# Expert weights in 2 KB packets, experts of the groups in turn, two scatters in flight

## The chip, the cores and the metric

The kernel runs on one core of one Trainium2 chip. The metric is the time of one execution on the device in microseconds (us). The profile is of one execution, taken by the hardware profiler; its times are microseconds from the span's start. PE is TensorE's matrix multiply, PEld its weight load, DVE is VectorE, ACT is ScalarE, POOL is GpSimd, SP is SyncE, which issues the ordinary DMAs; SPq and POOLq are sequencers. The core has 16 DMA engines, on which the DMAs of every issuing engine run: queue q1 holds what SP issues (plain loads and stores), q0 what GpSimd issues (indirect gathers and scatters).

## The reference

A decoder block on 1024 tokens of width 1024: a norm, a projection, stick-breaking attention beside a gated short convolution, merged and projected back, and then a mixture of experts. Only the last part is touched:

```python
def hierarchical_moe(h, w_rg, b_rg, w_re, b_re, w_gate, w_up, w_down):
    g_logits = hf @ w_rg + b_rg
    g_prob = jax.nn.softmax(g_logits, axis=-1)
    _, g_idx = lax.top_k(g_logits, 1)
    ...
    e_in_group = jnp.take_along_axis(e_logits, g_idx[:, :, None], axis=1)[:, 0]
    top_v, top_i = lax.top_k(e_in_group, TOP_K_IN_GROUP)
    ...
    for g in range(N_GROUPS):
        sl = slice(g * EXPERTS_PER_GROUP, (g + 1) * EXPERTS_PER_GROUP)
        act = silu(einsum('nd,edf->nef', h, w_gate[sl])) * einsum('nd,edf->nef', h, w_up[sl])
        act = act * combine[:, g, :, None]
        y = y + jnp.einsum('nef,efd->nd', act, w_down[sl])
```

There are 4 groups of 8 experts. A token takes one group and two experts in it, so that experts of different groups never share a token, while two of one group may. Gate and up are [1024, 256] each for an expert, down is [256, 1024], all float32: 3 MB an expert, 100 MB in all.

## The kernel before

Everything up to the merge is left as it is. The stages that matter begin at about 690 us.

**Output projection, second norm, routing** (from line 769). Eight tiles of 128 tokens. Tiles 0 to 5 run whole and end with `finish(t)` (L995): `add_x` adds the product to the residual rows XR[t % 3] on VectorE, `norm2` works out the norm's factor in small steps on GpSimd (L190 to L197), and `put_x(t, half)` (L866) multiplies one half of the row with the norm's gain into the buffer HX on GpSimd (L868) and issues two stores on SP: HX into the table h2d in DRAM (L869), XR into the output (L870). Tiles 6 and 7 run by column halves (L1020): `add_x` and `put_x` come after each half, and `norm2(6, G)` stands on GpSimd behind `put_x(6, 1)`. `tr_x`, `route`, `rank` and `table` (L880 to L956), spread over the products of later tiles, transpose the rows, choose group and experts, and build the slot tables: for each expert up to SLOTS = 88 rows with their token numbers. L1063 and L1064 turn them into `idx`; a slot without a token points to one of 128 rows past the output's end (`dumpc`, L780).

**Weight loads.** An expert has six chunks of 512 KB: four with 256 rows of gate and of up (two loads of 256 KB, L803), two with 128 rows of down (one load of 512 KB, L805). `chunks` (L790) fixes their order. `load_upto` (L807) issues loads on SP into a ring of some 39 buffers, CH, which come free one after the other as earlier stages end; in the expert loop a chunk is loaded again into a buffer once it has been split (L1112). A gate or up load takes rows i * 256 to i * 256 + 255: one contiguous run of 256 KB, which goes to the partitions in pieces of one row, 1 KB. A piece of down is 4 KB. A piece is a packet in the profile.

**Experts** (L1084 to L1198). Experts run in the order of their number. `gather(e)` fetches the expert's rows from h2d by `idx` (GpSimd, L1093). `xT` transposes them (PE L1134) and splits them in a high and a low part. `split_chunk` (L1100) splits each chunk alike: ScalarE copies the high part (L1103), VectorE subtracts (L1104). `expert_mm` does three products of 512 columns for each pair of parts (through `mm`, L124). `gateup(e)` runs four chunks, calls `aT(e - 1)`, `xT(e + 1)` and `gather(e + 3)` between them and ends with the activation; `down(e - 1)` follows, copies its result into one of two buffers YE (L1174) and issues the scatter that adds its rows to the output in DRAM (GpSimd, L1178). All scatters write the same tensor, so each waits on GpSimd until the one before has landed.

A loop for tokens past an expert's first 88 slots ends the kernel (L1212). With these inputs it runs no pass.

Of the kernel before, what the change touches and what calls it, by code (L numbers as in the profile page):

```python
# [40 lines left out]
class Order:  # L41
    """Puts steps given in a plain sequential order into the order in which to issue them: a step
    comes once what it reads is there and what it overwrites is read, the longest chain first."""
# [55 lines left out]
def tile_hybrid_block(  # L99
# [34 lines left out]
    def warm(n):  # L134
        """Products that nothing reads, to keep the array's clock up where it would idle."""
        for _ in range(n):
            mm(PS[:, 1, :], onesB, onesB[:, None, :].to_broadcast([128, 4, 128]), True, True)

    # ------------------------------------------------------------------ constants
# [62 lines left out]
    # ------------------------------------------------------------------ weights of three column blocks  # L202
# [35 lines left out]
    # ------------------------------------------------------------------ first norm, transposed  # L238
# [148 lines left out]
    def unit(n, u):  # L387
# [26 lines left out]
        def scan():  # L414
            P = PT[nP]
            # a first row block's last 128 keys of a diagonal unit are all masked
# [17 lines left out]
        for sp in range(w // 256):  # L434
            tr, x = 4 + state["sp"] % 2, state["sp"] % 3
            state["sp"] += 1
            # quarters (key block, row block); the masked one of a diagonal unit is zero
# [143 lines left out]
    # ------------------------------------------------------------------ transposed blocks of the other projections  # L581
# [186 lines left out]
    # ------------------------------------------------------------------ output projection, second norm, routing  # L768
# [11 lines left out]
    dumpc = rc.tile([128, 1], F32, name="dumpc")  # L780
    G.iota(dumpc, pattern=[[0, 1]], base=N + 1, channel_multiplier=1, allow_small_or_imprecise_dtypes=True)
# [7 lines left out]

    chunks = []  # L790
# [8 lines left out]
    def load_chunk(r, i, wg, wu, wd, Y=Y):  # L799
        if i < 4:  # L800
            v = r.rearrange("p (k j c) -> p k j c", k=2, j=2)
            for j, w in enumerate((wg, wu)):
                Y.dma_start(v[:, :, j], w[i * 256:(i + 1) * 256].rearrange("(k p) c -> p k c", p=128))  # L803
        else:
            Y.dma_start(r, wd[(i - 4) * 128:(i - 3) * 128])  # L805

    def load_upto(n, ring=0, Y=Y):  # L807
        while lst["n"] < min(n, len(chunks)):
            e, i = chunks[lst["n"]]
            load_chunk(CH[lst["n"] % (ring or len(chunks))], i, w_gate_e[0, e], w_up_e[0, e], w_down_e[0, e], Y)  # L810
# [55 lines left out]
    def put_x(t, half):  # L866
        tsl, hs = slice(t * 128, (t + 1) * 128), slice(half * 512, (half + 1) * 512)
        G.tensor_mul(HX[:, hs], XR[t % 3][:, hs], g2[:, hs])  # L868
        Y.dma_start(h2d[tsl, hs], HX[:, hs])  # L869
# [17 lines left out]
    def route(t):  # L887
# [27 lines left out]
        # combine weights times the norm's factor  # L915
# [103 lines left out]
    # the last two tiles by column halves  # L1019
# [41 lines left out]
    # slot tables  # L1061
    t2 = sm.tile([128, NE], F32, name="t2")
    V.tensor_scalar(t2[0:SLOTS], TAB[:, 0:NE], 0.0, dumpc[0:SLOTS], op0=OP.is_equal, op1=OP.mult)  # L1063
# [3 lines left out]
    # tiles past the first of each expert, as a running count  # L1067
# [15 lines left out]
    # ------------------------------------------------------------------ experts  # L1083
# [8 lines left out]
    def gather(e):  # L1092
        G.indirect_dma_start(out=XE[e % 2][:, :], out_offset=None, in_=h2d[:, :],  # L1093
                             in_offset=bass.IndirectOffsetOnAxis(ap=idx[0:SLOTS, e:e + 1], axis=0),
# [19 lines left out]
    def expert_mm(e, i, xt, at, o):  # L1114
        wh, wl = split.pop((e, i))
        if i < 4:
            for kk in range(2):
                k = 2 * i + kk
                cs = slice(kk * 512, (kk + 1) * 512)
                mm3(o, xt[0][:, k], xt[1][:, k], wh[:, cs], wl[:, cs], k == 0, k == 7)  # L1120
# [17 lines left out]
    pos = {"n": 0}  # L1138

    def gateup(e):  # L1140
# [14 lines left out]
        S.activation(sg, o[:, 0:DE], AF.Silu, scale=rsl[0:SLOTS, e:e + 1])  # L1155
        V.scalar_tensor_tensor(ac, o[:, DE:2 * DE], wsl[0:SLOTS, e:e + 1], sg, op0=OP.mult, op1=OP.mult)
# [10 lines left out]
    def down(e):  # L1167
# [10 lines left out]
        G.indirect_dma_start(out=out[:, :], out_offset=bass.IndirectOffsetOnAxis(ap=idx[0:SLOTS, e:e + 1], axis=0),  # L1178
# [101 lines left out]
```

## Time and profile before

| | us |
|---|---|
| runs | 1200.8, 1202.41, 1202.41 |
| median | 1202.41 |
| the profiled execution's span | 1199.3 |

| engine | busy us of the span | share |
|---|---|---|
| PE (products) | 1114.5 | 93% |
| PEld (weight loads) | 893.6 | 75% |
| DVE | 757.6 | 63% |
| ACT | 644.9 | 54% |
| POOL | 363.0 | 30% |

The profile has 149666 DMA packets with 169.18 MB, of which 129097 packets are under 2 KB. The span is the time from the first to the last event of the profiled execution; the runs are timed on their own. Busy shares are means over stages with different limits; what binds one stage is read in that stage. The DMA share is the time of all packets over the time of 16 engines, so that packets that overlap on an engine can bring it above 1.

### The profile page before, as it was taken

To read this page: it belongs to the slowest core of one execution; us is meant where nothing else is said; L and a number is where in the kernel's file an instruction comes from. 1 tells how busy PE (TensorE), PEld (TensorE's weight loads), DVE (VectorE), ACT (ScalarE), POOL (GpSimd) and SP (SyncE) were. 2 spreads that over 40 slices of the span, in tenths; PEclk is the share of its full clock that TensorE was granted. 3 is DMA by queue.
4 is the path that set the end of the run, shared out by engine and by line. 5 is a ranking of instruction groups with operands and counts; after the bars stand their busy time and mean duration, and the time that the engine had idled before them with its cause. 6 is when DMAs were issued, how large, how long until landed. Compare 5 with 4: busy or idle time off the path is not lost.

```text
span 1199.3 us, 16771 instructions
## 1 busy us (share of the span) xinstructions
PE 1114.5 (93%) x5761; PEld 893.6 (75%) x5761; DVE 757.6 (63%) x1317; ACT 644.9 (54%) x1204; POOL 363.0 (30%) x658
## 2 busy tenths in 40 slices
PE   6999898999999999999999999998899999899883
PEld 5988897987888888888888887786566656566552
DVE  5579989989885332333324073445598889688772
ACT  6586767777653213222223142223588878687672
POOL 4636466463000000000000004555363334333211
PEclk9999999998999999999999999999899999899897
DMA  6000101011011111111121168928899999999993
GB/s 222 27 27 14 40 2 40 15 29 34 1 36 54 53 36 45 53 53 52 37 62 45 36 189 290 322 73 276 241 316 312 323 323 292 310 314 317 328 322 82
DMA packets 149666, 169.18 MB, mean 141 GB/s; under 512 B 14381, under 2 KB 129097, under 8 KB 149577
## 3 DMA queue, kind: packets, MB, share of 16 engines
q1 hardware_dynamic: 140360, 148.12, 38.2%
q0 software_dynamic: 9216, 19.95, 7.7%
q8 instruction: 46, 0.75, 0.2%
q14 instruction: 44, 0.35, 0.1%
HBM read 150.72 MB, written 20.45 MB: 143 GB/s over the span
## 4 chain that ended last, share of the span: by engine, by line
PE 52%; DMA 27%; DVE 8%; issue 5%; POOL 4%; ACT 2%; SPq 1%; POOLq 0%; DVEq 0%; ACTq 0%
PE PS L124 49%; DMA out_dram<-xr,idx 10%; DMA out_dram<-ye,idx 8%; DVE pt L421 3%; PE PS L446 2%; DMA cha<-in_w_down_e_dram 2%; DMA xr<-h2d,idx 1%; DMA chr<-in_w_up_e_dram 1%; DVE WL L231 1%; DVE ahl L466 1%; POOL hx L868 1%; PE PS L338 1%; DMA chr<-in_w_down_e_dram 1%; DMA mg<-in_w_down_e_dram 1%; DMA h2d<-hx 1%
## 5 line engine op out<-in xcount | busy, mean ns | idle before, releaser
L124 PE MATMUL PS<-hH,WH 128*128 128x512 f32 x448 | 143.9, 394 | 1.1 <-DVE attF L478 1.1
L124 PE MATMUL PS<-hH,WL 128*128 128x512 f32 x448 | 142.0, 390 | 0.0
L124 PE MATMUL PS<-hL,WH 128*128 128x512 f32 x448 | 141.9, 389 | 0.0
L124 PE MATMUL PS<-WH,xet 128*88 128x512 f32 x384 | 137.9, 410 | 3.5 <-ACT WH L1103 3.5
L421 DVE TENSOR_TENSOR_SCAN pt<-pt 128x128 f32<-128x128 f32 (+2 forms) x96 | 92.8, 1008 | 18.5 <-issue 13.4
L674 POOL TENSOR_TENSOR mg<-mg,sga 128x1024 f32<-128x1024 f32 x6 | 14.7, 2456 | 293.0 <-DVE sga L672 293.0
L124 PEld LDWEIGHTS PS<-hH,WL 128*128 128x128 f32 x448 | 84.1, 188 | 17.7
L124 PEld LDWEIGHTS PS<-hH,WH 128*128 128x128 f32 x448 | 84.1, 188 | 17.4 <-ACT WH L610 1.2
L124 PEld LDWEIGHTS PS<-hL,WH 128*128 128x128 f32 x448 | 84.2, 188 | 16.4
L124 PE MATMUL PS<-WH,hH 128*128 128x384 f32 x256 | 91.9, 359 | 4.4 <-ACT hH L268 2.3
L611 DVE SCALAR_TENSOR_TENSOR WL<-br,cols,WH 128x128 fp32r<-128x128 f32 x200 | 68.9, 411 | 29.3 <-ACT WH L610 29.3
L124 PE MATMUL PS<-WH,hL 128*128 128x384 f32 x256 | 87.2, 341 | 0.0
L124 PE MATMUL PS<-WL,hH 128*128 128x384 f32 x256 | 86.8, 339 | 0.0
L615 DVE TENSOR_TENSOR WL<-br,WH 128x512 fp32r<-128x512 f32 x16 | 11.1, 691 | 116.5 <-ACT WH L614 116.5
L610 ACT ACTIVATE WH<-br,cols 128x128 fp32r<-128x128 f32 x200 | 65.4, 392 | 35.6 <-PE PS L124 34.4
L124 PE MATMUL PS<-WL,xet 128*88 128x512 f32 x192 | 79.2, 413 | 4.9 <-DVE WL L1104 4.4
L124 PEld LDWEIGHTS PS<-WH,xet 128*88 128x88 f32 x384 | 61.3, 160 | 29.5 <-ACT WH L1103 4.1
L124 PE MATMUL PS<-WH,act 128*88 128x512 f32 x192 | 65.5, 395 | 1.2 <-ACT act L1164 1.2
L1178 POOL DMA_INDIRECT out_dram<-xr,idx x16 | 35.2, 2200 | 100.7 <-DMA out_dram<-ye,idx 56.0
L460 POOL CAST ahl<-zeros 128x256 fp32r<-128x256 f32 x32 | 30.4, 958 | 115.5 <-PE PS L124 107.0
L124 PE MATMUL PS<-ahl,vt 128*128 128x256 f32 x320 | 53.7, 298 | 11.4 <-DVE attF L478 10.7
L1178 POOL DMA_INDIRECT out_dram<-ye,idx x16 | 31.5, 1970 | 99.6 <-DMA out_dram<-xr,idx 75.7
(278 smaller groups left out, 2726.2 us busy)
## 6 DMA issues: line engine op xcount, KB each, us to landing
br<-in_w_in_dram SPq DMA_DIRECT2D x25, 512.0 KB
cha<-in_w_gate_e_dram SPq DMA_DIRECT2D x42, 256.0 KB
cha<-in_w_up_e_dram SPq DMA_DIRECT2D x42, 256.0 KB
cha<-in_w_down_e_dram SPq DMA_DIRECT2D x18, 512.0 KB
mg<-in_w_down_e_dram SPq DMA_DIRECT2D x17, 512.0 KB
mg<-in_w_gate_e_dram SPq DMA_DIRECT2D x29, 256.0 KB
mg<-in_w_up_e_dram SPq DMA_DIRECT2D x29, 256.0 KB
br<-in_w_in_dram SPq DMA_DIRECT2D x36, 192.0 KB
```

The source lines that it names most:

```text
L124: T.matmul(o, a, b, start=start, stop=stop)
L231: V.scalar_tensor_tensor(WL3[:, k], WR[idx, k // 2][:, k % 2], g1[:, k:k + 1], WH3[:, k], op0=OP.mult, op1=OP.subtract)
L338: T.transpose(pb[:, j].bitcast(F32R), st[:, a, j * 128:(j + 1) * 128], identR)
L421: V.tensor_tensor_scan(pr, pr, pr, 1.0 if diag else P[:, j, w:w + 1], op0=OP.mult, op1=OP.bypass)
L446: T.transpose(PS[:, tr, q * 128:(q + 1) * 128], BT[n % 3][:, j, (sp * 2 + sj) * 128:(sp * 2 + sj + 1) * 128], identF)
L460: G.tensor_copy(AHL[x][:, :, 0:128], zeros[:, None, :].to_broadcast([128, 2, 128]))
L466: V.tensor_sub(AHL[x][:, 1, lo:512], PS[:, tr, lo:512], AHL[x][:, 0, lo:512])
L610: S.activation(j.wH[:, k], r[:, k], AF.Copy, scale=g1[:, k:k + 1])
L611: V.scalar_tensor_tensor(j.wL[:, k], r[:, k], g1[:, k:k + 1], j.wH[:, k], op0=OP.mult, op1=OP.subtract)
L674: (G if b < 6 else V).tensor_add(mg, mg, mst[b].rearrange("p (t c) -> p t c", c=128))
L868: G.tensor_mul(HX[:, hs], XR[t % 3][:, hs], g2[:, hs])
L1178: G.indirect_dma_start(out=out[:, :], out_offset=bass.IndirectOffsetOnAxis(ap=idx[0:SLOTS, e:e + 1], axis=0), in_=ye[:, :], in_offset=None ...
```

## The change

1. A gate or up load now takes two neighbouring rows for each partition: partition p holds rows 8p to 8p + 7, chunk i rows 8p + 2i and 8p + 2i + 1. A piece is 2 KB, and the pieces of a load lie 8 KB apart in DRAM. The columns of h2d are stored in the matching order (k, p) in place of (p, k), so that `xT` still takes 128 neighbouring columns. In `put_x` both products on GpSimd come with the second half, read in steps of 8 elements, and one store writes the whole row. In the chunk gate and up lie as (j k c), and a product reads gate and up of one k as two runs of 256 columns.
2. Experts run in the order EX: one of group 0, one of group 1, 2, 3, then the second of each group, and so on. Slots without a token point into one half or the other of the spare rows, by the parity of the group, so that neighbouring scatters share no row.
3. The dependency of a scatter on the one just before is taken away, and one on the scatter two before is set. Ahead of the last four a memset of one element stands on GpSimd.

The rest of the diff takes comments out and follows the new names.

```diff
-    dumpc = rc.tile([128, 1], F32, name="dumpc")
-    G.iota(dumpc, pattern=[[0, 1]], base=N + 1, channel_multiplier=1, allow_small_or_imprecise_dtypes=True)
+    dumpc = rc.tile([128, 2], F32, name="dumpc")
+    G.iota(dumpc[:, 0:1], pattern=[[0, 1]], base=N + 1, channel_multiplier=1, allow_small_or_imprecise_dtypes=True)
+    G.iota(dumpc[0:64, 1:2], pattern=[[0, 1]], base=N + 65, channel_multiplier=1, allow_small_or_imprecise_dtypes=True)
+    G.iota(dumpc[64:128, 1:2], pattern=[[0, 1]], base=N + 1, channel_multiplier=1, allow_small_or_imprecise_dtypes=True)
...
+    EX = [(n % 4) * 8 + n // 4 for n in range(NE)]
...
         if i < 4:
-            v = r.rearrange("p (k j c) -> p k j c", k=2, j=2)
+            v = r.rearrange("p (j k c) -> p j k c", k=2, j=2)
             for j, w in enumerate((wg, wu)):
-                Y.dma_start(v[:, :, j], w[i * 256:(i + 1) * 256].rearrange("(k p) c -> p k c", p=128))
+                Y.dma_start(v[:, j], w.rearrange("(p k) c -> p k c", k=8)[:, 2 * i:2 * i + 2])
...
-        G.tensor_mul(HX[:, hs], XR[t % 3][:, hs], g2[:, hs])
-        Y.dma_start(h2d[tsl, hs], HX[:, hs])
+        if half:
+            for q in range(2):
+                c = slice(q * 512, (q + 1) * 512)
+                G.tensor_mul(HX.rearrange("t (k p) -> t k p", k=8)[:, :, q * 64:q * 64 + 64],
+                             XR[t % 3][:, c].rearrange("t (p k) -> t k p", k=8), g2[:, c].rearrange("t (p k) -> t k p", k=8))
+            Y.dma_start(h2d[tsl, :], HX)
         Y.dma_start(out[tsl, hs], XR[t % 3][:, hs])
...
-    V.tensor_scalar(t2[0:SLOTS], TAB[:, 0:NE], 0.0, dumpc[0:SLOTS], op0=OP.is_equal, op1=OP.mult)
+    for v in range(2):
+        V.tensor_scalar(t2[0:SLOTS].rearrange("p (h v e) -> p v h e", h=2, v=2)[:, v],
+                        TAB.rearrange("p (h v e) -> p v h e", h=2, v=2)[:, v], 0.0, dumpc[0:SLOTS, v:v + 1], op0=OP.is_equal, op1=OP.mult)
...
         if i < 4:
+            wh, wl = [w.rearrange("p (j k c) -> p k j c", k=2, j=2) for w in (wh, wl)]
+            o = o.rearrange("p (j c) -> p j c", j=2)
             for kk in range(2):
                 k = 2 * i + kk
-                cs = slice(kk * 512, (kk + 1) * 512)
-                mm3(o, xt[0][:, k], xt[1][:, k], wh[:, cs], wl[:, cs], k == 0, k == 7)
+                mm3(o, xt[0][:, k], xt[1][:, k], wh[:, kk], wl[:, kk], k == 0, k == 7)
...
-        G.indirect_dma_start(out=out[:, :], out_offset=bass.IndirectOffsetOnAxis(ap=idx[0:SLOTS, e:e + 1], axis=0),
-                             in_=ye[:, :], in_offset=None, compute_op=OP.add)
+        if e + 4 >= NE:
+            G.memset(gap, 0.0)
+        SCAT.append(G.indirect_dma_start(out=out[:, :], out_offset=bass.IndirectOffsetOnAxis(ap=idx[0:SLOTS, EX[e]:EX[e] + 1], axis=0),
+                                         in_=ye[:, :], in_offset=None, compute_op=OP.add).ins)
+
+        if e:
+            tc.declare_no_dep(SCAT[e], SCAT[e - 1], reason="rows of different groups")
+        if e >= 2:
+            tc.add_manual_dep(SCAT[e], SCAT[e - 2].name, mybir.DependencyInfo(mybir.DependencyClass.Sync, mybir.DependencyReason.DATA),
+                              reason="the rows before")
```

## Rows read from the trace of the kernel before

**Rows 1.** page, span and what the DMA engines moved in 40 equal slices (GB/s)

```profile
span 1199.3 us, 16771 instructions
...
GB/s 222 27 27 14 40 2 40 15 29 34 1 36 54 53 36 45 53 53 52 37 62 45 36 189 290 322 73 276 241 316 312 323 323 292 310 314 317 328 322 82
```

**Rows 2.** stretches: busy us of PE, PEld, DVE, ACT, POOL; clock, DMA share, GB/s

```profile
890.00:925.00 35.00, 35.00 (x179) 24.14 (x178) 32.45 (x41) 31.76 (x43) 13.68 (x7) 1.00 1.06 305
...
995.00:1030.00 35.00, 30.76 (x153) 20.35 (x151) 26.58 (x32) 26.66 (x36) 18.79 (x8) 0.98 1.01 303
...
1100.00:1135.00 35.00, 29.82 (x132) 19.28 (x131) 24.84 (x30) 24.51 (x33) 10.15 (x8) 0.90 1.06 327
```

**Rows 3.** chain of waits, 865 to 1100 us: start, us, what

```profile
869.52 8.95 DMA out_dram<-xr,idx
...
1012.80 14.34 DMA out_dram<-xr,idx
...
1078.89 9.44 DMA out_dram<-xr,idx
```

**Rows 4.** waits of ScalarE, 855 to 1075 us: total us, times, longest

```profile
ACT xr L1174 <- DMA out_dram<-xr,idx: 15.4, 6, 6.1
ACT ye L1174 <- DMA out_dram<-ye,idx: 8.5, 5, 2.9
```

**Rows 5.** waits of ScalarE, 1075 to 1175 us, the longest

```profile
ACT hw L1103 <- DMA cha<-in_w_up_e_dram: 5.5, 2, 3.4
```

**Rows 6.** DMA queues, 855 to 1165 us: packets, MB, share of 16 engines

```profile
q1 hardware_dynamic: 62418, 79.44, 78.3%
q0 software_dynamic: 8388, 18.13, 26.5%
```

**Rows 7.** load queue in 725-731, 917-919, 739.3-741.7, 14.5-17.5 and 626-630 us

```profile
q1 hardware_dynamic: 2331, 2.26, 107.6%
...
q1 hardware_dynamic: 797, 0.77, 109.2%
...
q1 hardware_dynamic: 525, 0.98, 105.5%
...
q1 hardware_dynamic: 347, 1.26, 103.0%
...
q1 hardware_dynamic: 1040, 0.52, 46.3%
```

**Rows 8.** stretches as in rows 2, before the first gather

```profile
840.00:845.00 5.00, 4.91 (x16) 2.15 (x16) 3.56 (x4) 0.22 (x1) 4.01 (x4) 0.59 0.31 122
```

**Rows 9.** timeline: start, us, engine, line, operation (TensorE, one chunk)

```profile
1101.50 1.60 PE L124 MATMUL PS<-hw,xet 128*88 128x512 f32 x6
```

**Rows 10.** timeline of the tail; in brackets the idle time before and its releaser

```profile
1177.82 1.56 POOL L1178 DMA_INDIRECT out_dram<-xr,idx  x1 [6.20 <-ACT act L1164]
...
1180.59 0.69 DVE L1177 COPY ye<-PS 88x512 f32<-88x512 f32 x1 [2.74 <-PE PS L124]
...
1185.69 1.57 POOL L1178 DMA_INDIRECT out_dram<-ye,idx  x1 [6.31 <-DMA out_dram<-xr,idx]
```

**Rows 11.** timeline of GpSimd ahead of the first gather

```profile
821.96 1.29 POOL L868 TENSOR_TENSOR hx<-xr,g 128x512 f32<-128x512 f32 x1 [0.68 <-DVE xr L863]
...
833.80 1.27 POOL L868 TENSOR_TENSOR hx<-xr,g 128x512 f32<-128x512 f32 x1 [2.38 <-DVE nrA L199]
...
840.01 3.66 POOL L945 TENSOR_TENSOR oha<-oha,ohs 128x32 f32<-128x32 f32 x1
...
844.86 1.31 POOL L1093 DMA_INDIRECT xr<-h2d,idx  x1 [0.92 <-issue]
```

**Rows 12.** groups of GpSimd, 690 to 850 us: busy us, mean ns

```profile
L868 POOL TENSOR_TENSOR hx<-xr,g 128x512 f32<-128x512 f32 x16 | 20.2, 1281 | 7.1 <-DMA h2d<-hx 3.5 <-DVE nrA L199 2.4 <-DVE xr L863 0.7
```

**Rows 13.** page, costliest groups: two of GpSimd

```profile
L674 POOL TENSOR_TENSOR mg<-mg,sga 128x1024 f32<-128x1024 f32 x6 | 14.7, 2456 | 293.0 <-DVE sga L672 293.0
...
L460 POOL CAST ahl<-zeros 128x256 fp32r<-128x256 f32 x32 | 30.4, 958 | 115.5 <-PE PS L124 107.0
```

More of the change, by code (lines that the diff above doesn't have):

```diff
@@ L809, in load_upto @@
             e, i = chunks[lst["n"]]
-            load_chunk(CH[lst["n"] % (ring or len(chunks))], i, w_gate_e[0, e], w_up_e[0, e], w_down_e[0, e], Y)
+            load_chunk(CH[lst["n"] % (ring or len(chunks))], i, w_gate_e[0, EX[e]], w_up_e[0, EX[e]], w_down_e[0, EX[e]], Y)
             lst["n"] += 1
@@ L1093, in gather @@
         G.indirect_dma_start(out=XE[e % 2][:, :], out_offset=None, in_=h2d[:, :],
-                             in_offset=bass.IndirectOffsetOnAxis(ap=idx[0:SLOTS, e:e + 1], axis=0),
+                             in_offset=bass.IndirectOffsetOnAxis(ap=idx[0:SLOTS, EX[e]:EX[e] + 1], axis=0),
                              bounds_check=N - 1, oob_is_err=False)
@@ L1138, in tile_hybrid_block @@
     pos = {"n": 0}
+    SCAT = []
+    gap = me.tile([1, 1], F32, name="gap")
     def gateup(e):
@@ L1154, in gateup @@
                 split_upto(pos["n"] + 3)
-        S.activation(sg, o[:, 0:DE], AF.Silu, scale=rsl[0:SLOTS, e:e + 1])
-        V.scalar_tensor_tensor(ac, o[:, DE:2 * DE], wsl[0:SLOTS, e:e + 1], sg, op0=OP.mult, op1=OP.mult)
+        S.activation(sg, o[:, 0:DE], AF.Silu, scale=rsl[0:SLOTS, EX[e]:EX[e] + 1])
+        V.scalar_tensor_tensor(ac, o[:, DE:2 * DE], wsl[0:SLOTS, EX[e]:EX[e] + 1], sg, op0=OP.mult, op1=OP.mult)
         split_upto(pos["n"] + 3)
@@ L1228, in tile_hybrid_block @@
         V.tensor_copy(wx[0:SLOTS, 0:3], PS[0:SLOTS, 7, 0:3])
-        V.tensor_scalar(wx[0:SLOTS, 3:4], wx[0:SLOTS, 0:1], 0.0, dumpc[0:SLOTS], op0=OP.is_equal, op1=OP.mult)
+        V.tensor_scalar(wx[0:SLOTS, 3:4], wx[0:SLOTS, 0:1], 0.0, dumpc[0:SLOTS, 0:1], op0=OP.is_equal, op1=OP.mult)
         V.scalar_tensor_tensor(ix[0:SLOTS], wx[0:SLOTS, 0:1], -1.0, wx[0:SLOTS, 3:4], op0=OP.add, op1=OP.add)
@@ L1247, in tile_hybrid_block @@
         S.activation(YE[0], PS[0:SLOTS, 2:4, :].rearrange("p b c -> p (b c)"), AF.Copy)
-        G.indirect_dma_start(out=out[:, :], out_offset=bass.IndirectOffsetOnAxis(ap=ix[0:SLOTS, 0:1], axis=0),
-                             in_=YE[0][:, :], in_offset=None, compute_op=OP.add)
+        last = G.indirect_dma_start(out=out[:, :], out_offset=bass.IndirectOffsetOnAxis(ap=ix[0:SLOTS, 0:1], axis=0),
+                                    in_=YE[0][:, :], in_offset=None, compute_op=OP.add).ins
+        tc.add_manual_dep(last, SCAT[NE - 2].name, mybir.DependencyInfo(mybir.DependencyClass.Sync, mybir.DependencyReason.DATA),
+                          reason="the rows before")
     for q in (me, xop, cha, rc, mgp, hTp, vtp, brp, wp, consts, dram, psum):
```

## The prediction

> **What bounds the kernel now.** I read the page's slices first. From the 29th of 40 on, the cores' DMA moves 241 to 328 GB/s until the last slice [rows 1]: the expert stage, from about 850 us, is the place to look. The table by stretches shows a DMA share of 1.06, 1.01 and 1.06 there, early, in the middle and late, while TensorE's busy time falls from 35.00 of 35 us to 29.82 [rows 2]. A share above 1 means that packets of two queues overlap a little; the 16 engines have nothing left.
>
> The chain of waits tells another story: from 865 to 1089 us it is scatter after scatter, each issued when the one before has landed. From 869.52 to 1078.89 there are 22 of them, 9.52 us an expert [rows 3]. A reader who stops here takes that as the bound. But what does ScalarE, which splits every weight chunk, wait for? From 855 to 1075 for scatters that still read its output buffer (15.4 and 8.5 us in total) and never for a weight load [rows 4]; after 1075 loads lead its list (5.5 us the first entry) [rows 5]. So the experts run at 9.5 us and eat up the chunks that were loaded ahead, and once that lead is gone the loads set the pace. How fast are the loads? In 310 us their queue moved 79.44 MB [rows 6]; an expert has 3.15 MB of weights (8 gate and up loads of 256 KB, two down loads of 512 KB), so 12.3 us an expert. They were never idle in that time, so the stage ends where it starts plus this work. **The DMA engines bound the expert stage; the scatter chain only hides that in its first two thirds.**
>
> **Gate and up in 2 KB packets.** Today a packet has 1 KB, for two thirds of the bytes. The price of a size is read where only that size runs. 1 KB loads (725 to 731 us): 107.6% of 16 engines for 6 us is 103.3 us of engine time for 2.26 MB, 45.7 us a MB, at 377 GB/s; in the expert stage, in 2 us that no scatter or gather disturbs, 0.77 MB, 385 GB/s. 2 KB (739.3 to 741.7): 105.5% of 2.4 us is 40.5 us for 0.98 MB, 41.3 us a MB, 408 GB/s. 4 KB loads: 49.4 us for 1.26 MB, 39.2 us a MB, 420 GB/s [rows 7]. The 2 KB row is of stores, not loads; it lies between the two rows of loads, nearer to 4 KB, as a fixed cost of each packet would have it.
>
> The stage loads 2/3 of 79.44 = 53.0 MB of gate and up. By engine time: 45.7 - 41.3 = 4.4 us a MB; in the stage everything is dearer (78.3% of 16 x 310 us is 3884 us for 79.44 MB, 48.9 us a MB, against 43.5 for the undisturbed mix: a factor of 1.12), so 53.0 x 4.4 x 1.12 / 16 = 16.3 us of all engines, 15.6 us of time at a share of 1.05. By rate: 53.0 x (1/377 - 1/408 GB/s) = 10.7 us; with 385 for 377, 7.7 us. I take **12 us less**, between rate and engine time, and keep 7.7 and 15.6. An expert's loads then need 12.3 - 12/25 = 11.8 us. What is loaded before 850 us gains nothing: the engines have room there (a share of 0.31 from 840 to 845 [rows 8]), the loads wait for free buffers.
>
> The product that now reads a chunk in two runs of 256 columns instead of one of 512 has as many columns. No row shows such a read; I take nothing. TensorE's six products start 0.24 us apart at most (1.60 us, the last one 0.40 [rows 9]), 36 of them and the transposes make some 9.1 us an expert; a tenth more on the 24 that change gives 9.7, still under 11.8.
>
> **Two scatters at once, groups in turn.** The removed wait lets the experts go from 9.5 towards 9.1 us. Then the lead runs out sooner, and **in the stage that buys nothing**: next in line is the load, as it is now after 1075. At most it fills the stretch where the share fell to 1.01: 35 x 0.045 = 1.6 us; I take 0. It does pay **at the tail**: the last scatter is issued at 1185.69, after the landing of the one issued at 1177.82, though its rows were ready at 1181.28 (1180.59 + 0.69) [rows 10]. After, it needs only the scatter two before: issue at about 1181.5, **4.2 us less**; if the two hinder each other, half of it, 2 us. Behind two scatters in GpSimd's queue stands the next gather; it is issued two experts (18 us) ahead of its use, and a scatter takes 9 to 10, so it is covered; without the cover TensorE would pay, which has 2.7 us an expert to spare. The four one-element memsets, the second table operation and the two more iotas are 0.1 to 0.25 us each; only the table (0.25) is on the path.
>
> **The permuted rows.** This is the cost. GpSimd's two products of a tile read in steps of 32 bytes, and both now come after the second half. For tiles 0 to 5 one store of 512 KB replaces two, SP issues eight DMAs fewer, and GpSimd has idle time between tiles. For tile 6 the products stand on GpSimd ahead of the norm which releases the routing: before, one, of 1.29 us at 821.96 [rows 11]. No row shows a product with such steps. Contiguous it is 1.28 us (16 of them) [rows 12]; GpSimd's dearest row by element is the cast of 256 in 0.958 us, 1.92 us for 512, and the product of twice the size took 2.46 [rows 13]. So the routing comes later by 2 x 1.28 - 1.29 = 1.3 to 2 x 2.46 - 1.29 = 3.6 us; with 1.92, which I take since it is a row of this size's cost per element, 2.55. For tile 7 the pair stands on GpSimd ahead of the last routing's small steps and of the first gather (833.80, 840.01, 844.86 [rows 11]): started at 833.8, it ends at 837.6 instead of 835.07, also 2.6 later, side by side with the other delay. With the table's 0.25 I take **3.2 us more** (ends 1.5 and 5.5). The loads that follow the first gathers move with them, so it is paid in full. The Trainium skill (GPSIMD Engine Reference, section 7, Performance pitfalls for Q7 kernels) states half as much again for reads in steps over 8 bytes; by it 1.92 us too, and no run here shows it yet.
>
> **The sum.** 1199.3 - 12 - 4.2 + 3.2 = 1186.3 us of span. The runs shown, 1200.8 to 1202.41, lie 1.5 to 3.1 us above the profiled span; from their median, 1202.4 - 13.0 = **1189.4**. Own range: 1202.4 - 15.6 - 4.2 - 1.6 + 1.5 = 1182.5 to 1202.4 - 7.7 - 2 + 5.5 = 1198.
>
> **The rivals.**
> (a) The packets gain nothing, because bytes bound the stage, or because the two rows are not joined into one packet: 1202.4 - 4.2 + 3.2 = 1201.4. For it: with all queues at work the engines move 315 GB/s, well under both rates [rows 6]. Against: 377 and 408 on the same engines [rows 7]. The Trainium skill (DMA: Bandwidth & Descriptors, Specifications) gives 512 B as the least transfer for line rate; that is this rival, and the rows of 512 B, 1 KB and 4 KB (57, 45.7 and 39.2 us a MB [rows 7]) disagree. 12 in 100.
> (b) Slower: a load of one run of 256 KB becomes 128 pieces 8 KB apart, and the memory answers such steps worse. At 0.7 us a MB above today's price the gain of the tail is gone and the kernel 0.2% slower; at 50 us a MB, 53.0 x 4.3 x 1.12 / 16 / 1.05 = 15 us more than today's loads, 1217. Against it: pieces of 512 B, 20 KB apart in in_w_in, take 46.3% of 4 us, 29 ns each, and a line through 1 KB and 4 KB gives 28 [rows 7]. 8 in 100.
> (c) Slower too: a product with steps costs 5 us, not 1.9 (GpSimd took 3.66 us for a small addition at 840.01 [rows 11], where VectorE was at work). Then the pairs of tiles 6 and 7 come in a row, 8.7 and 8 us, and the start moves by 16 and eats all: 1202.4 and more, from about 4.7 us a product on. 5 in 100.
> (d) More: engine time counts in full, the share is refilled, the start costs 1.5: 1182.5 and below, to 1179. 8 in 100.
>
> **How the numbers follow.** The forecast has 67 in 100. 0.2% is 2.4 us, about what a measurement of this kernel can tell from no change; of (a)'s twelve, eight lie within it and four on the fast side. Faster 0.67 + 0.08 + 0.04 = 0.79, same 0.08, slower 0.13. The range takes in (a) and a part of (d) and leaves out (b) and (c): 1181.5 to 1202.5.
>
> **What would show it.** Right: gate and up in packets of 2 KB near 41 us a MB; more than 325 GB/s in the stage with the share still above 1; ScalarE waiting for loads earlier than 1075; no scatter waiting for the one just before; the last one issued within 1 us of its rows. Wrong: a share below 0.95 in the stage (then scatters, gathers or TensorE bound it), a 2 KB price above 45, or a first gather later than 850.5 us.

## The result, and the profile after

After the change the kernel takes 1210.59 us (median of 4 runs, 1209.51 to 1211.03), 1.0061 times the time before, with a 95% interval of 1.0045 to 1.0077: slower by some 7.3 us, where 1189.4 was forecast.

The page, span and what the DMA engines moved in 40 slices (as rows 1):

```profile
span 1208.7 us, 16757 instructions
...
GB/s 221 27 27 21 33 2 40 15 44 19 1 36 70 35 35 53 53 44 53 53 58 39 52 204 264 304 79 246 222 318 300 303 297 300 311 321 326 307 346 122
```

Stretches (as rows 2): us, then busy us of PE, PEld, DVE, ACT, POOL; clock, DMA share, GB/s.

```profile
890.00:925.00 35.00, 35.00 (x179) 24.16 (x178) 33.30 (x41) 31.79 (x43) 20.05 (x8) 1.00 1.05 307
995.00:1030.00 35.00, 32.75 (x159) 21.53 (x157) 27.78 (x35) 26.69 (x36) 10.09 (x7) 1.00 1.03 303
1100.00:1135.00 35.00, 29.60 (x129) 18.38 (x128) 24.93 (x30) 23.81 (x33) 9.60 (x6) 0.90 1.03 321
```

DMA queues from 855 to 1165 us (as rows 6):

```profile
q1 hardware_dynamic: 35102, 76.77, 75.3%
q0 software_dynamic: 8496, 18.14, 26.8%
```

The packets of q1 fell from 62418 to 35102: the two rows are joined, as meant. But the stage is no quicker. The three stretches move 307, 303 and 321 GB/s where they moved 305, 303 and 327, and the share is 1.05, 1.03 and 1.03 where it was 1.06, 1.01 and 1.06. The engines are as busy as before with fewer packets; each has become dearer than its size says.

What ScalarE waits for from 855 to 1075 us (as rows 4): total us, times, longest.

```profile
ACT xet L1148 <- PE PS L1147: 16.0, 17, 8.9
ACT hw L1115 <- DMA cha<-in_w_up_e_dram: 3.8, 2, 2.9
```

The waits for scatters (15.4 and 8.5 us) are gone, and loads stand in the list that held none: the experts eat up their lead sooner, as foretold, and then wait for weights. (Of the first entry, 8.9 us are the wait for the first transposes, ahead of the first expert.)

GpSimd ahead of the first gather (as rows 11; start, us, engine, line, operation):

```profile
821.91 2.00 POOL L877 TENSOR_TENSOR hx<-xr,g 128x512 f32<-128x512 f32 x1
...
839.74 4.02 POOL L877 TENSOR_TENSOR hx<-xr,g 128x512 f32<-128x512 f32 x2 [1.01 <-DMA h2d<-hx]
...
854.42 1.31 POOL L1105 DMA_INDIRECT xr<-h2d,idx  x1 [0.21 <-issue]
```

The first gather stands at 854.42 where it stood at 844.86 [rows 11]: 9.6 us late, with 3.2 forecast. A product in steps takes 2.0 us, as forecast.

The tail (as rows 10):

```profile
1190.66 1.57 POOL L1195 DMA_INDIRECT out_dram<-xr,idx  x1 [6.72 <-ACT act L1179]
...
1193.67 0.69 DVE L1192 COPY ye<-PS 88x512 f32<-88x512 f32 x1 [2.72 <-PE PS L124]
...
1195.18 1.58 POOL L1195 DMA_INDIRECT out_dram<-ye,idx  x1 [2.92 <-ACTq L1235]
```

The last scatter is issued 0.8 us after its rows (1193.67 + 0.69) instead of 4.4 us after them [rows 10]. From there to the span's end it is 13.5 us, before 13.6: the two last scatters don't hinder each other.

So three of the four terms have to be found again: the packets, the stage with two scatters, the start.

### The profile page after: what moved, and what is told of

It is laid out like the page before. It is cut to its first block, busy times and chain, and to the rows that moved or that the text cites. A ratio compares the mean times of both kernels' runs of the same rounds, so it can differ in the third digit from the quotient of the medians.

```text
span 1208.7 us, 16757 instructions
## 1 busy us (share of the span) xinstructions
PE 1119.9 (93%) x5761; PEld 896.4 (74%) x5761; DVE 767.0 (63%) x1318; ACT 648.5 (54%) x1204; POOL 366.0 (30%) x664
## 5 line engine op out<-in xcount | busy, mean ns | idle before, releaser
L1105 POOL DMA_INDIRECT xr<-h2d,idx x32 | 47.4, 1482 | 63.3 <-PE PS L1147 62.5
L124 PE MATMUL PS<-ahl,vt 128*128 128x256 f32 x320 | 53.8, 298 | 11.3 <-DVE attF L478 10.6
L124 PE MATMUL PS<-hw,xet 128*88 128x512 f32 x192 | 55.7, 420 | 7.9 <-DVE hw L1116 4.7
```

The source lines that it names most:

```text
L124: T.matmul(o, a, b, start=start, stop=stop)
```

## The experiments

Ratios are to the kernel before, with 95% intervals; 0.1% is 1.2 us. Where two runs are compared, it is by their ratios; such a difference is sure to 3 or 4 us to either side (the two intervals added as squares), so that one under 3 us isn't clear of noise. A single profile's start can lie 2 to 3 us to either side (the first gathers of experiments 7, 9 and 11, which are alike up to there, lie at 842.5 to 846.2 us), so that times from one profile are read with that in mind.

**1. Rows stored as before.** The changed kernel, with the table's rows in their old order; `xT` picks its columns in steps of 8.

```diff
-        if half:
-            for q in range(2):
...
+        G.tensor_mul(HX[:, hs], XR[t % 3][:, hs], g2[:, hs])
+        Y.dma_start(h2d[tsl, hs], HX[:, hs])
...
-                T.transpose(pb[:, k], xe[:, kk * 128:(kk + 1) * 128], identF[0:SLOTS, 0:SLOTS])
+                T.transpose(pb[:, k], xe.rearrange("s (p k) -> s k p", k=8)[:, kk], identF[0:SLOTS, 0:SLOTS])
```

> The changed kernel, but the rows are stored as before (a product of contiguous columns and a store for each half) and the transposes of the experts read the columns in steps of 8 instead. Loads of 2 KB and the two scatters in flight stay. Theory A (the permuted rows start the expert stage some 10 us later, and the rest of the change is worth next to nothing): about 1200.5, first gather near 845 us, 1 KB and 2 KB alike in the stage. Theory B (it is the 8 KB steps of the loads or the scatters that cost): stays at 1207 or more, though the first gather is back at 845. Theory C (the forecast's 12 us are there and only hidden): 1189.

Measured: 1202.24 us, ratio 0.9994 (0.9972 to 1.0015), first gather at 846.78. Against the changed kernel that is 0.67%, **8.1 us for the permuted rows alone** (4.9 to 11.3). That is theory A. TensorE's transposes take longer in steps, 272 ns each where they took 245 (232 of them from 860 to 1160 us are 29.8 us of TensorE's time instead of 23.5), 0.2 us an expert; what that does to the kernel's time no run shows by itself. And everything else together, packets, order, two scatters and tail, comes to nothing that can be told from noise.

**2. The scatters alone.** The kernel before with groups in turn and two scatters; loads and rows as before.

```diff
+            tc.declare_no_dep(SCAT[e], SCAT[e - 1], reason="rows of different groups")
```

> Only the order of the groups and the two scatters in flight; loads of 1 KB from contiguous 256 KB and rows as before. Theory A (the stage is bound by the loads, so only the tail gains): 1197 to 1200. Theory D (with two scatters in flight the scatters take more from the loads than one does, 12 us in the stage): 1208 to 1213. If the pace of the experts had been the bound after all: 1190 or less.

Measured: 1202.98 us, 1.0004 (0.9983 to 1.0025). That is between the two theories. The tail's gain is in it (rows to issue 0.8 us), so something in the stage takes as much again.

**3. The packets alone.** The kernel before with the changed loads, and `xT` as in 1; scatters in series, experts by number.

```diff
+                Y.dma_start(v[:, j], w.rearrange("(p k) c -> p k c", k=8)[:, 2 * i:2 * i + 2])
```

> Only the loads of 2 KB in steps of 8 KB, transposes in steps of 8; rows stored as before, scatters one after the other, experts in number order. Theory A (beside scatters and gathers the size of a packet doesn't matter): 1201 to 1204. The forecast's price of a packet: 1190. Theory B (steps of 8 KB are answered worse): 1206 or more. A difference between 1190 and 1201 says what share of the 12 us is real.

Measured: 1197.15 us, 0.9959 (0.9938 to 0.998): 4.9 us (2.4 to 7.5), less than half of the forecast 12.

**4. Place without steps.** The changed kernel with both products after the second half and one store, but the products contiguous.

```diff
-                G.tensor_mul(HX.rearrange("t (k p) -> t k p", k=8)[:, :, q * 64:q * 64 + 64],
...
+                G.tensor_mul(HX[:, c], XR[t % 3][:, c], g2[:, c])
```

> The changed kernel with both products still after the second half and one store of 512 KB, but of contiguous columns (1.28 us each instead of 2.00); the transposes read in steps of 8. It parts the price of the steps from that of the place. If the steps of the product cost the start: near the kernel of e1, 1202 to 1203. If the place (two products ahead of the norm, one store at the end) costs: 1206 to 1209, the first gather only 1.5 to 3 us earlier than in the changed kernel.

Measured: 1203.67 us, 1.0007 (0.9984 to 1.0029), first gather at 848.43: the steps cost 6.5 us (the changed kernel against this one), the place some 1.6 (against 1), which is within the noise.

**5. Steps without the place.** The changed kernel with each product in steps back after its own half; still one store. (HX is one buffer, so half of tile 6's row in the table is overwritten by tile 7's here; no time hangs on the values.)

```diff
+        G.tensor_mul(HX.rearrange("t (k p) -> t k p", k=8)[:, :, half * 64:half * 64 + 64],
+                     XR[t % 3][:, hs].rearrange("t (p k) -> t k p", k=8), g2[:, hs].rearrange("t (p k) -> t k p", k=8))
```

> The changed kernel, with each product in steps of 8 back in its old place, one after each half of a row, and still one store a row. Theory A, a product in steps holds up VectorE's small steps beside it, in every tile, so that the start comes later by the steps and not by the place: first gather 852 to 854, 1208 to 1210. Rival B, what costs is that the pairs of tiles 6 and 7 stand ahead of the norm and the routing: first gather 847 to 848, 1203 to 1205.

Measured: 1209.85 us, 1.0063 (1.0043 to 1.0084), first gather at 853.75. Theory A holds: putting the products back brings nothing. The price is that of the steps.

**6. Prices by themselves.** A kernel of loads and small steps only.

```diff
+    for kind in range(3):
+        beside(kind)
...
+    phase(6, 1, down=False)
+    phase(6, 2, down=False)
+    phase(6, 3, down=False)
+    phase(6, 1)
+    phase(6, 2)
+    phase(6, 3)
+    phase(8, 1, scat=1, nscat=7)
...
+    phase(8, 1, scat=2, nscat=14)
```

> Leaves out the whole block: it only loads expert weights, phase by phase, with and without scatters of 88 rows, ahead of which GpSimd's products run beside small steps of VectorE; its time says nothing. Gate and up alone in 1 KB packets, in 2 KB packets 8 KB apart, in 2 KB packets out of one run; then the same three with down between. Theory A, a packet's price sets the rate: 377, 408, 408 GB/s, with down 390 and 411. Rival B, something below the packets' price sets it (bytes, or how many loads are under way): all within 2% of each other. Loads with one scatter under way: by the expert stage 290 to 300 GB/s of loads and scatter together, at 1 KB and 2 KB alike; by A 3% apart. With two under way: fewer bytes of load than with one, if two scatters slow the loads (5 us in 310 found); the same if they only move work. Scatters that write without adding: if adding is what is dear, the loads come back to the rate that they have alone. Loads issued by two engines: if the number under way is the limit, over 3% faster than by one. VectorE's small steps: 0.2 us each alone; beside a product of GpSimd, theory C (VectorE stands still for it) up to the product's length, 1.3 us contiguous and 2.0 us in steps; rival D, 0.2 us in all three.

VectorE's timeline: eight additions of two tensors of 128 x 32 (L80), then eight steps with one tensor (L82): first alone, then beside six contiguous products of GpSimd, then beside six in steps.

```profile
5.54 1.78 DVE L80 TENSOR_TENSOR sc<-sa,sb 128x32 f32<-128x32 f32 x8
7.35 1.70 DVE L82 TENSOR_SCALAR sc<-sa 128x32 f32<-128x32 f32 x8
...
13.75 6.70 DVE L80 TENSOR_TENSOR sc<-sa,sb 128x32 f32<-128x32 f32 x8
20.49 2.64 DVE L82 TENSOR_SCALAR sc<-sa 128x32 f32<-128x32 f32 x8
...
27.83 10.36 DVE L80 TENSOR_TENSOR sc<-sa,sb 128x32 f32<-128x32 f32 x8
38.23 3.36 DVE L82 TENSOR_SCALAR sc<-sa 128x32 f32<-128x32 f32 x8
```

GpSimd in the same time:

```profile
13.62 8.17 POOL L74 TENSOR_TENSOR hx<-xa,ga 128x512 f32<-128x512 f32 x6 [13.17 <-DVE xa L71]
27.76 12.49 POOL L76 TENSOR_TENSOR hx<-xa,ga 128x512 f32<-128x512 f32 x6 [5.97 <-DVE xa L71]
```

An addition takes 0.22 us alone, on the mean 0.84 beside contiguous products and 1.30 beside products in steps: theory C. Taken singly, an addition that falls between two products takes 0.19 us, and one that meets a product takes 1.14 to 1.30 us, in steps 1.86 to 2.02: it ends with the product. Of the steps with one tensor only one meets a product, the last of the six, and takes 1.12 and 1.84 us; the others take 0.18. So VectorE stands still while GpSimd's product runs, and a longer product holds it longer. The Trainium skill (SBUF — State Buffer, section Who interferes with whom) says it: a VectorE instruction with two inputs in SBUF contends with a GpSimd instruction that reads SBUF. This trace agrees, 0.22 against 0.84 and 1.30 us. In the changed kernel the same is seen in the routing. VectorE, then GpSimd with the products and the routing's next step of its own:

```profile
744.89 1.97 DVE L920 TENSOR_TENSOR OH<-iot,ge 128x64 f32<-128x64 f32 x1
746.90 1.87 DVE L922 TENSOR_TENSOR ohs<-OH 128x32 bf16<-128x32 f32 x1
```

```profile
744.79 3.93 POOL L877 TENSOR_TENSOR hx<-xr,g 128x512 f32<-128x512 f32 x2
748.69 0.28 POOL L926 TENSOR_SCALAR s<-m 128x1 f32<-128x1 f32 x1
```

The same place in the kernel before, VectorE and GpSimd:

```profile
743.91 0.99 DVE L904 TENSOR_SCALAR pen<-iog,s 128x32 f32<-128x32 f32 x1
744.93 1.22 DVE L905 TENSOR_TENSOR pen<-pen,lg 128x32 f32<-128x32 f32 x1
...
746.92 0.23 DVE L910 TENSOR_TENSOR OH<-iot,ge 128x64 f32<-128x64 f32 x1
747.18 0.19 DVE L912 TENSOR_TENSOR ohs<-OH 128x32 bf16<-128x32 f32 x1
```

```profile
743.58 2.52 POOL L868 TENSOR_TENSOR hx<-xr,g 128x512 f32<-128x512 f32 x2
746.07 0.24 POOL L916 TENSOR_SCALAR s<-m 128x1 f32<-128x1 f32 x1
```

There the products held two other steps (0.24 and 0.19 us in the changed kernel). The four steps together took 2.63 us before and 4.27 after, 1.6 more; the pair of products itself takes 1.4 more.

VectorE isn't the only one that is held. The step `s<-m` stands on GpSimd right behind the products, and ScalarE waits for it with the routing's exponentials. ScalarE's wait from 735 to 822 us (total, times, longest), before and after, then TensorE's wait for VectorE's `ohs`:

```profile
ACT s L917 <- POOL s L916: 37.8, 6, 7.4
ACT s L927 <- POOL s L926: 45.5, 6, 9.5
```

```profile
PE PS L124 <- DVE ohs L912: 2.7, 2, 1.5
PE PS L124 <- DVE ohs L922: 4.1, 2, 2.2
```

Followed back from the first gather, from releaser to releaser, the chain of experiment 5 runs, among others, through four pairs of products of tiles 0 to 5, 15.8 us, and that of experiment 1 through the same four, 10.1 us: 5.7 of the 7.0 us between their first gathers. In the changed kernel it runs through two such pairs and several steps of VectorE that were held. So the longer product reaches the first gather on both ways, over GpSimd's own next step and over VectorE; no run parts them.

Now the loads. Stretches in the middle of a phase (us, busy us of VectorE and GpSimd, clock, DMA share, GB/s): gate and up alone in packets of 1 KB, of 2 KB lying 8 KB apart, of 2 KB out of one run; the same three with down; then 1 KB and 2 KB 8 KB apart beside scatters in series.

```profile
98.00:122.00 24.00, 2.61 (x17) 0.00 (x0) 1.00 1.07 374
139.00:172.00 33.00, 2.14 (x14) 0.00 (x0) 1.00 1.00 354
186.00:212.00 26.00, 0.15 (x1) 0.00 (x0) 1.00 1.01 390
228.00:270.00 42.00, 0.00 (x0) 0.00 (x0) 1.00 1.06 392
285.00:333.00 48.00, 0.00 (x0) 0.00 (x0) 1.00 1.00 341
350.00:390.00 40.00, 0.00 (x0) 0.00 (x0) 1.00 1.04 408
412.00:458.00 46.00, 0.00 (x0) 8.16 (x11) 1.00 1.06 351
498.00:545.00 47.00, 0.61 (x4) 8.13 (x10) 1.00 1.02 322
```

Theory A is right for packets out of one run, 374 to 390 and 392 to 408 GB/s. **Lying 8 KB apart, 2 KB packets are slower than 1 KB packets**: 354 and 341. The last line beside the one above it says the same with scatters in series, 322 against 351. Two more phases had two scatters under way and moved 319 and 320 GB/s, but with a scatter every 4.5 to 4.6 us instead of every 9 to 10, so they don't part number from overlap; experiment 12 does. The phases with two engines issuing and with scatters that don't add give no rate: loads of the second engine ran ahead into the phase before and mixed them. A packet's price can still be read: a 4 KB row that a scatter adds took 329 to 347 ns, one that it only writes 184.

**7. Contiguous pairs.** The kernel of experiment 1, but a 2 KB packet takes rows 256i + 2p and 256i + 2p + 1, so that a load is one run of 256 KB again; `xT` picks its columns to match.

```diff
-                Y.dma_start(v[:, j], w.rearrange("(p k) c -> p k c", k=8)[:, 2 * i:2 * i + 2])
+                Y.dma_start(v[:, j], w[i * 256:(i + 1) * 256].rearrange("(p k) c -> p k c", k=2))
...
-                T.transpose(pb[:, k], xe.rearrange("s (p k) -> s k p", k=8)[:, kk], identF[0:SLOTS, 0:SLOTS])
+                T.transpose(pb[:, k], xe.rearrange("s (i p k) -> s i k p", k=2, p=128)[:, kk // 2, kk % 2], identF[0:SLOTS, 0:SLOTS])
```

> As the run with rows stored as before, groups in turn and two scatters (1202.2), with one difference: a 2 KB packet now takes two neighbouring rows out of one run of 256 KB, so that a load's packets no longer lie 8 KB apart. Theory A, the steps of 8 KB cost nothing and something else eats two thirds of the forecast gain: 1202 +- 1.5. Rival B, the steps of 8 KB eat the rest of the packets' gain (12 forecast, some 4 found): the loads of the stage take some 8 us less, 1194 to 1196.

Measured: 1198.09 us, 0.9966 (0.9951 to 0.9982): 3.4 us better than with 8 KB between packets (0.2 to 6.6). Rival B has the sign, and half of its size.

**8. Only the last scatter free.** Experiment 3, experts in turn by groups, and of all waits of a scatter for the one before only the last taken away.

```diff
+        if e == NE - 1:
+            tc.declare_no_dep(SCAT[e], SCAT[e - 1], reason="rows of different groups")
+            tc.add_manual_dep(SCAT[e], SCAT[e - 2].name, mybir.DependencyInfo(mybir.DependencyClass.Sync, mybir.DependencyReason.DATA),
+                              reason="the rows before")
```

> The kernel with 2 KB packets alone (1197.2), with the experts in turn by groups, and the last scatter alone freed of the one before; all others stay in series, rows are stored as before. Theory A, the tail's gain is had without the stage's loss: 1197.2 - 3.6 = 1193.6. Rival B, the last two scatters hinder each other: half of it, 1195.4. Rival C, the order by groups itself slows the loads (by the 5 us put down to two scatters): 1198 to 1199.

Measured: 1195.33 us, 0.9938 (0.9915 to 0.9961). Rival C falls: the order by groups costs nothing that shows; A and B can't be told apart. It differs from experiment 1 in that its other scatters stay in series (and in the place of the one-element memsets), and is 0.56% (6.7 us) quicker.

**9. Both.** Experiment 8 with the pairs of 7, run beside 10.

```diff
-                Y.dma_start(v[:, j], w.rearrange("(p k) c -> p k c", k=8)[:, 2 * i:2 * i + 2])
+                Y.dma_start(v[:, j], w[i * 256:(i + 1) * 256].rearrange("(p k) c -> p k c", k=2))
```

> The kernel of the last free scatter (1195.3), with the 2 KB packets of a load taken out of one run of 256 KB in place of 8 KB apart; rows of the table stay as before, and xT reads them in steps of 2. Theory A, the steps of 8 KB cost some 4 us beside serial scatters as they do beside two (1202.2 against 1198.1): 1191.2. Rival B, the steps cost only where two scatters are under way: 1195.

Measured: 1190.41 us, **0.9886 (0.986 to 0.9912): 13.7 us quicker than before**, the best of all. The time is that of theory A; its reason, the steps of 8 KB, is looked at behind experiment 11.

**10. The tail alone.** Experiment 8 with loads and `xT` of the kernel before.

```diff
-                Y.dma_start(v[:, j], w.rearrange("(p k) c -> p k c", k=8)[:, 2 * i:2 * i + 2])
+                Y.dma_start(v[:, :, j], w[i * 256:(i + 1) * 256].rearrange("(k p) c -> p k c", p=128))
```

> The kernel before (1202.2), with the experts in turn by groups, and the last scatter alone freed of the one before; loads stay in 1 KB packets. Theory A, the tail gives what its wait shows, from 4.4 us between rows and issue to 1: 1198.8. Rival B, the last two scatters hinder each other and half of it comes: 1200.4.

Measured: 1197.36 us, 0.9953 (0.993 to 0.9976): 5.7 us by the ratio, 2.9 to 8.4 by its interval. Theory A. Experiment 9 against it prices the contiguous packets at 8.1 us; experiment 8 against it the packets 8 KB apart at 1.8, within the noise. Experiment 2 against it prices the other two-at-once scatters at 6.1 us **more**.

**11. Two scatters at the pace of one.** Experiment 7 with two products more for each expert, which nothing reads.

```diff
+            if e >= 3 and i < 2:
+                mm(PS[:, 7, :], onesB, onesB[:, None, :].to_broadcast([128, 4, 128]), True, True)
```

> The kernel with 2 KB packets out of one run, groups in turn and two scatters (1198.1), with two more products of 512 columns for each expert from the fourth on, which nothing reads (some 0.45 us of TensorE), so that the experts go at the pace of serial scatters (9.2 to 9.6 us) while two scatters may still be under way. Theory A, two scatters spread over more of the time and so hold up the loads: the loads of the stage stay at 308 us, 1198 or 1 to 2 more. Rival B, the quicker pace is what costs (more scatters and gathers early, the lead used up sooner): the loads come back to 304 us, 1193 to 1195.

Measured: 1200.28 us, 0.999 (0.9977 to 1.0003). From the issue of the 37th chunk's load to that of the 187th, 25 experts, it is 311.8 us, 308.4 in experiment 7, 303.8 in experiment 9. From the fourth activation to the 20th the experts went at 9.85 us (9.40 in experiment 7), no quicker than with serial scatters (9.72 in experiment 9), and the loads didn't come back. Rival B falls: it isn't the pace. The same stretch in the other runs, us in one profile of each:

| loads of gate and up | scatters in series | two under way |
|---|---|---|
| 1 KB | before 309.1; experiment 10, 309.0 | experiment 2, 313.9 |
| 2 KB, 8 KB apart | experiments 3 and 8, 304.4 and 303.4 | experiment 1, 309.3; changed kernel, 311.5 |
| 2 KB out of one run | experiment 9, 303.8 | experiment 7, 308.4 |

In this stretch two scatters cost some 5 us in each form, and 2 KB bring some 5 whichever way they lie. So what the steps of 8 KB cost the kernel (3.4 us by 7 against 1, 6.2 by 9 against 8, each just clear of noise) doesn't show here. Ahead of the first gather the loads run without scatters, as in experiment 6 where the steps do cost; that they cost it there isn't shown.

From 855 to 1155 us, experiments 9, 7 and 11:

```profile
855.00:1155.00 300.00, 290.08 (x1381) 197.58 (x1380) 252.19 (x311) 243.53 (x327) 98.72 (x58) 0.99 1.03 321
```

```profile
855.00:1155.00 300.00, 285.24 (x1351) 195.54 (x1350) 248.48 (x304) 245.29 (x320) 89.89 (x58) 0.99 1.03 314
```

```profile
855.00:1155.00 300.00, 290.33 (x1396) 193.87 (x1395) 249.27 (x304) 243.49 (x320) 87.17 (x58) 1.00 1.03 310
```

At the same share, 321, 314 and 310 GB/s. Where does it go? From the packet records of 862 to 1150 us one can count at each moment how many packets of gathers and scatters were under way on the 16 engines. Time with none, of 288 us:

| scatters | kernels | us with none under way |
|---|---|---|
| in series | before; experiments 3, 8, 9, 10 | 86.0; 86.4, 87.3, 82.0, 85.5 |
| two | after; experiments 1, 2, 7, 11 | 73.9; 69.0, 70.5, 67.4, 61.2 |

With none under way the loads of experiment 7 move 360 GB/s, with one to four of these packets 272, with five to eight 207, with more 148. Two scatters spread the same packets over more of the time, and the time with none is where the loads are quickest. As an estimate: put experiment 9's shares of time in these four bands in place of experiment 7's, each band at experiment 9's rate, and the loads move 1.0 MB more in the 288 us; measured are 1.9 MB more (74.5 against 72.6). So the spread goes with the loss and accounts for about half of it by this count; what takes the rest stays open.

**12. Two scatters, same number.** Loads of twelve experts a phase, one scatter for each expert in series, or two together for every second.

```diff
+    for form in (1, 3):
+        phase(12, form, 1, False)
+        phase(12, form, 2, False)
+        phase(12, form, 1, True)
+        phase(12, form, 2, True)
+    phase(12, 2, 1, True)
```

> Leaves out the whole block: it loads the weights of twelve experts a phase; its time says nothing. A scatter of 88 rows belongs to each expert, issued when the expert's first chunk is there, in series; or two together for every second expert, so that the number is the same and two are under way at once. Both without and with a gather for each expert, with 1 KB packets and with 2 KB packets out of one run; at last 2 KB packets 8 KB apart, in series, with gathers. Theory A, two scatters under way make the other packets dearer: with pairs the loads move 2% less, and the 4 KB packets of down cost 5% more (181 to 192 ns in the expert stage). Rival B, only their number per time matters: the same with pairs and in series. Theory C, beside scatters and gathers contiguous 2 KB packets still gain 3 to 4% on 1 KB, and lose as much 8 KB apart. Rival D, the scatters and gathers set the rate: all within 2%.

The phases, 37.75 MB of loads each, so that their length (second column) is the price: 1 KB in series, in pairs; the same with gathers; 2 KB out of one run, the same four; 2 KB lying 8 KB apart in series with gathers.

```profile
54.20:177.50 123.30, 2.74 (x28) 19.58 (x24) 1.00 1.04 341
185.60:309.40 123.80, 3.65 (x49) 19.42 (x23) 1.00 1.04 338
317.80:464.10 146.30, 4.85 (x56) 33.38 (x36) 1.00 1.05 317
472.90:616.60 143.70, 3.98 (x42) 33.30 (x37) 1.00 1.06 320
625.60:746.50 120.90, 2.86 (x30) 19.46 (x24) 1.00 1.03 347
754.80:875.50 120.70, 3.49 (x46) 19.42 (x23) 1.00 1.02 347
884.00:1029.80 145.80, 4.57 (x51) 33.42 (x36) 1.00 1.02 319
1037.40:1182.20 144.80, 5.25 (x63) 33.27 (x36) 1.00 1.03 318
1191.30:1338.30 147.00, 4.04 (x43) 33.42 (x36) 1.00 1.02 315
```

Theory A falls and rival B holds here: in pairs it takes as long as in series, with gathers even 2.6 and 1.0 us less. Two under way are not dear as such. Counted as above, pairs issued together leave 67.0 us without packets of scatters and gathers where series leave 55.7 (with gathers, 1 KB): here they spread over less time, in the kernel over more, and the price has the sign of the spread in both. Why they come so in the kernel was not tried, and no run changed the spread alone, so that it is the cause is argued and not shown. On the packets rival D holds: beside scatters and gathers all three forms take 145.8 to 147.0 us. In the kernel 2 KB brought some 5 us in the 25 experts of the table above, and out of one run 4.6 to 8.1 in all (7 against 2, 9 against 10), more than the 0.5 in 146 here for twelve; what makes that difference stays open.

## Why the prediction was wrong

**What bounds the stage** was right: the share stays at 1.03 to 1.05, no gain comes from the experts' quicker pace, and ScalarE waits for loads earlier. Three smaller readings were wrong and left the sum as it is. From 869.52 to 1078.89 us there are 21 scatters, so an expert took 10.5 us and not 9.52, still less than its loads. A share above 1 doesn't need two queues: q1 alone shows 107.6% [rows 7]. And in rival (b), 0.7 us a MB above today's price makes the kernel 1.5 us slower with the tail and the start counted, 0.1% and not 0.2%.

**The packets, 12 us forecast, 1 to 5 found** (experiments 3, 8 against 10, 1 against 2). Two steps of the working failed. The price of 2 KB was read where neither scatters nor gathers ran; beside them nearly all of the difference is gone in the kernel of loads (145.8 against 146.3 us), and in the 25 experts over which the working spread its 12 us, some 5 were found, for either form of 2 KB. And the row for 2 KB was one of stores. Out of one run, loads alone bear it out (390 and 408 GB/s); 8 KB apart, loads alone of 2 KB cost about what 1 KB costs or more (341 and 354 GB/s). That is rival (b), which had 8 in 100 and no end near 0: I asked whether it would turn a gain into a loss, not whether it would eat a part of the gain. Out of one run the packets bring 4.6 to 8.1 us, about the lower end of 7.7. By the rule of the Trainium skill (DMA: Bandwidth & Descriptors, Specifications: line rate from 512 B) nothing was to be had: the loads alone disagree with it (374 and 390 GB/s), the loads beside scatters and gathers come within 1% of it.

**Two scatters, 0 forecast in the stage, 6 to 7 us of loss found** (2 against 10, 1 against 8; 9.7 for 7 against 9). The step "in the stage that buys nothing: next in line is the load" asked only what a freed wait could gain. The scatters run on the same 16 engines as the loads that bound the stage, and how they lie in time changes what the loads get: 308 to 314 us for the loads of 25 experts instead of 303 to 309. That the loss comes with two under way is shown; by what way is argued (behind experiment 11). I had no row with two under way, and took 0 without a lower end for it.

**The tail, 4.2 us forecast**, was right: 3.6 us between rows and issue in the profile, 5.7 (2.9 to 8.4) in time.

**The start, 3.2 us forecast, 8.1 found.** The product's price was right, 2.0 us by a forecast of 1.92, and so was the rule of the Trainium skill cited for it (GPSIMD Engine Reference, section 7, Performance pitfalls for Q7 kernels: half as much again; 1.28 to 2.01 us). The step that failed is the cover, for tiles 0 to 5: "GpSimd has idle time between tiles". It has, but not where it is needed: right behind a tile's products stands GpSimd's own step of the routing, for which ScalarE waits (45.5 us in all instead of 37.8 from 735 to 822), and beside them VectorE's small steps stand still (four of them 4.27 us instead of 2.63). So the delay grew tile by tile: in experiment 5 VectorE's additions to the residual rows of tiles 2 to 5 come 3.4, 3.7, 3.9 and 5.3 us later than in experiment 1, and the first gather 7.0. Of the 8.1 us, 6.5 are the steps and only 1.6 the place that I had costed, and that is within the noise. Rival (c) had the sign and the place right, and the mechanism wrong; it needed products of 4.7 us.

The sum with what was found: -3 for the packets, -5 for the tail, +6.5 for the scatters, +8.1 for the rows, together +6.6; measured +7.3. Each of these is sure to 2 to 4 us, so that they meet so closely is partly luck.

Of the signs that the prediction named as wrong, two came: a first gather later than 850.5 us, and a price of 2 KB packets above 45 us a MB (99.7 ns a packet from 855 to 1165 us, 48.7 us a MB; 1 KB before, 51.7 ns, 50.5). Of those named as right, the 41 us a MB and the 325 GB/s did not come; ScalarE's earlier waits for loads and the last scatter within 1 us of its rows did.

## What to carry to other kernels

An engine's idle time covers a longer instruction only if nothing that another engine waits for stands behind it, and no other engine is held up beside it: look at the next step in its queue and at what the neighbour does in those microseconds. Where the DMA engines bound a stage, a wait between transfers may be what keeps them apart; free only the wait that ends last, here the last scatter's. Read a packet's price where the same other queues run and the same steps in DRAM are taken, and put neighbouring rows into a packet without spreading the packets of a load.

## What the runs showed of the hardware

- Loads alone, of 2 KB packets 8 KB apart: 341 to 354 GB/s; out of one run: 390 to 408; 1 KB out of one run: 374 to 392 (experiment 6). In the expert stage, with scatters in series, both forms of 2 KB took 303 to 304 us for 25 experts, 1 KB 309.
- A small VectorE addition that meets a product of GpSimd ends with it: 1.14 to 1.30 us instead of 0.19, and 1.86 to 2.02 where the product reads in steps of 32 bytes; a step with one tensor that met one took 1.12 and 1.84 us instead of 0.18. A product in such steps takes 2.01 us, contiguous 1.28.
- A scatter and a gather for each expert's 3.15 MB of loads take the loads' rate from 373 GB/s (a whole phase of experiment 6, 18.9 MB in 50.6 us) to 258 (37.75 MB in 146.3 us) with 1 KB packets.
- Two scatters issued together cost no more than two in series (143.7 and 146.3 us for the same work); in the kernel, where two left 61 to 74 us of 288 without packets of scatters and gathers and series 82 to 87, the loads of 25 experts took some 5 us longer with two.
- A 4 KB row took 329 to 347 ns of a DMA engine where a scatter adds it to DRAM, and 184 where it only writes it.
- TensorE's transposes of an expert's rows took 272 ns where they read in steps of 8 elements, contiguous 245.
